# ConvFFN of a hybrid decoder layer: a small product that nothing reads, of eleven kinds in turns, behind every tenth group of projection matmuls

## The chip, the cores and the metric

The kernel runs on one core of one Trainium2 chip. The metric is the device time of one execution in microseconds, as the median of several runs. A core has five engines that run side by side and meet through semaphores: TensorE (PE) multiplies matrices and writes to PSUM, VectorE (DVE) and ScalarE (ACT) compute element by element, GpSimd (POOL) does small copies and issues DMAs, SyncE (SP) issues DMAs. PEld is the part of TensorE that loads the stationary operand (the weights) of a product ahead of its turn.

## The reference

One inference step of one layer, for a prompt of 256 tokens and for 8 samples of 4 tokens; 256 + 32 = 288 token columns go through the projections together. The layer has a Mamba-2 branch and a gated linear attention branch, a merge, cross-attention into 256 memory tokens, and a causal ConvFFN. The change touches the last part alone:

```python
up = _rmsnorm(h, p['norm_ffn']) @ p['w_up']                 # 2048 -> 2 * 5632
up, ffn_conv_new = _causal_dwconv(up, ffn_conv, p['ffn_conv_w'], p['ffn_conv_b'])
a, gt = jnp.split(up, 2, axis=-1)
h = h + (jax.nn.silu(gt) * a) @ p['w_down']                 # 5632 -> 2048
```

All weights and results are fp32. The outputs are y for both groups of tokens, the new convolution and recurrent states and the memory keys and values.

## The kernel before, in words

Every projection goes through `proj_w`. It takes a strip of 256 output channels (two groups of 128, `j`), walks over the inner dimension in tiles of 128 rows, and adds into two PSUM tiles `acc`, each 128 channels by 288 tokens. The weights come as 512 KB loads (`raw`, three buffers, issued by SP). `wsplit` turns each pair of tiles into two fp32r parts: `hi` by a cast on ScalarE (L102, tile whi) and `lo`, the rest, by a subtraction on VectorE (L104, tile wlo), with five buffers each. The activations are split in the same way (hf for the up-projection, pr for the down-projection).

One step of the generator is one pair of inner tiles. For each of the two groups `j` it makes six products of 128 weight columns by 288 token columns: hi by high part (L134) and hi by low part (L135) for both inner tiles, then lo by high part (L138) for both. So a step is 12 products, in the order 134 135 134 135 138 138, twice. At the end of a step the generator yields.

The ConvFFN is a loop over six blocks of channels. `ffn_up` runs the strips of w_up of a block (inner dimension 2048, 8 steps each), and as each strip ends `ffn_conv` does the convolution on VectorE, ScalarE and GpSimd; `ffn_down` runs the 8 strips of w_down for the block before (4 steps each, 2 for the first and smaller block). `flush` puts work that was set aside, such as the transposes of the convolution caches (L1540), into a strip's second half; in the last block `tail_rows` (L1619) transposes finished rows for the output. PSUM has eight banks: four for acc, three for `mm`, one for `la`, which cross-attention used last.

The kernel asks for a schedule that is made with a simulated timeline; `tc.keep_in_program_order` ties an instruction to its place among its engine's instructions.

Of the kernel before, what the change touches and what calls it, by code (L numbers as in the profile page):

```python
# [16 lines left out]
P = 128  # L17
# [24 lines left out]
def hybrid_step(ctx: ExitStack, tc: tile.TileContext, I: dict, O: list):  # L42
# [4 lines left out]
    MM, TR = nc.tensor.matmul, nc.tensor.transpose  # L47
# [12 lines left out]
    def acc_tiles(n):  # L60

        turn[0] += 1
        return [ps.tile([P, 512], F32, tag=f"acc{turn[0] % 2}", bufs=2, name="acc") for _ in range(n)]
# [4 lines left out]
    def la_tile():  # L68
        return ps.tile([P, 512], F32, tag="la", bufs=1, name="la")


    ident = const.tile([P, P], F32, name="ident")
    make_identity(nc, ident)
    ones = const.tile([P, P], F32, name="ones")
# [24 lines left out]
    def wsplit(raw):  # L99

        hi = wp.tile(list(raw.shape), F32R, tag="whi", bufs=WB, name="whi")
        S.copy(hi, raw)  # L102
        lo = wp.tile(list(raw.shape), F32R, tag="wlo", bufs=WB, name="wlo")
        V.tensor_tensor(lo, raw, hi, ALU.subtract)  # L104
        return hi, lo
# [4 lines left out]
        return raw  # L110

    late = []

    def flush():

        while late:
            late.pop(0)()

    def proj_w(load, ncol, X, nk, cons, N=T):

        nt = (ncol + P - 1) // P
        accs = acc_tiles(nt)
        for k0 in range(0, nk, 4):
            kn = min(4, nk - k0)
            raw = load(k0, kn)
            for s0 in range(0, kn, 2):
                hi, lo = wsplit(raw[:, s0:s0 + 2, :])
                for j in range(nt):
                    m = min(P, ncol - j * P)
                    a = accs[j][0:m, 0:N]  # L130
                    cs = slice(j * P, j * P + m)
                    for k in range(2):
                        xh, xl = X(k0 + s0 + k)
                        MM(a, hi[:, k, cs], xh, start=(k0 + s0 + k == 0), stop=False)  # L134
                        MM(a, hi[:, k, cs], xl, start=False, stop=False)  # L135
                    for k in range(2):
                        xh, xl = X(k0 + s0 + k)
                        MM(a, lo[:, k, cs], xh, start=False, stop=(k0 + s0 + k == nk - 1))  # L138
                    if k0 + s0 + 2 == nk:
                        cons(j, a)  # L140
                if k0 + s0 == min(4, nk - 2):
                    flush()
                yield

    def proj(w, c0, ncol, X, nk, cons, row0=0):
        def load(k0, kn):
            return wload(w[row0 + k0 * P:row0 + (k0 + kn) * P, c0:c0 + ncol].rearrange("(k p) n -> p k n", p=P))
        return proj_w(load, ncol, X, nk, cons)
# [41 lines left out]
    def halves(alloc, name):  # L190

        ts = [alloc(f"{name}{i}") for i in range(2)]

        def at(k, n=None):
            t, o = ts[k // 8], k % 8
            if n is None:
                return t[:, o, :], t[:, 8 + o, :]
            return t[:, o:o + n, :], t[:, 8 + o:8 + o + n, :]
        return at
# [52 lines left out]
    X = halves(bigr, "xn")  # L252
    with pool("p0") as p0:
# [227 lines left out]
        def dt_cons(j, a):  # L481
# [4 lines left out]
            V.tensor_tensor(lr3[64:80, :], a[64:80], lr3[64:80, :], ALU.subtract)  # L486

        run(proj_w(dt_load, 112, X, KT, dt_cons))

        def dt_prep():  # L490
# [737 lines left out]
    for q in range(4):  # L1228
        m = pc.tile([P, 4, T], F32, tag="mar", bufs=2, name="mar")
# [36 lines left out]
    def rstd_of():  # L1266
        ssq = mm_tile()
        MM(ssq[:, 0:T], ones, rst.pop(), start=True, stop=True)
        return rstd_from(pb, ssq[:, 0:T], D)
# [4 lines left out]
    for j2 in range(KT // 2):  # L1274
        def cons(j, a, j2=j2):
            added(hx[j2][:, j, :], 2 * j2 + j, a, vec("norm_cross"), hn, acc)
# [236 lines left out]
    rf = []  # L1513
    store = []

    def ffn_conv(ct, a, out, st, cache):
        if not rf:
            rf.append(rstd_of())
        u = pf.tile([P, SEQ], F32, tag="fu", bufs=3, name="fu")
        sp = pf.tile([P, NB, 6], F32, tag="fsp", bufs=4, name="fsp")  # L1520
        G.tensor_copy(sp[:, :, 0:2], st.rearrange("p (b k) -> p b k", k=2))
        V.tensor_tensor(u, a[:, 0:SEQ], rf[0][:, 0:SEQ], ALU.mult)
        V.tensor_tensor(sp[:, :, 2:6], a[:, SEQ:T].rearrange("p (b l) -> p b l", l=NL),
                        rf[0][:, SEQ:T].rearrange("p (b l) -> p b l", l=NL), ALU.mult)
        w2, wb = fcol[:, 2, ct:ct + 1], fcol[:, 3, ct:ct + 1]
        S.activation(out[:, 0:SEQ], u, ACT.Identity, scale=w2, bias=wb)
        S.copy(cache[:, 0:2], u[:, SEQ - 2:SEQ])
        S.copy(cache[:, 2:18].rearrange("p (b k) -> p b k", k=2), sp[:, :, 4:6])
        outs = out[:, SEQ:T].rearrange("p (b l) -> p b l", l=NL)
        V.tensor_scalar(outs, sp[:, :, 2:6], w2, wb, ALU.mult, ALU.add)  # L1530
        for k in range(2):
            s = 2 - k
            V.scalar_tensor_tensor(outs, sp[:, :, k:k + 4], fcol[:, k, ct:ct + 1], outs, ALU.mult, ALU.add)
            V.scalar_tensor_tensor(out[:, s:SEQ], u[:, 0:SEQ - s], fcol[:, k, ct:ct + 1], out[:, s:SEQ], ALU.mult, ALU.add)
# [16 lines left out]
    def ffn_up(b0, n):  # L1551
        pr = bigr2("pr")
        todo = []
        for q0 in range(b0, b0 + n, 4):
            st = fst[:, q0 // 4]
            ca = pf.tile([P, 18, 4], F32, tag="fca", bufs=3, name="fca")
            cg = pf.tile([P, 18, 4], F32, tag="fcg", bufs=3, name="fcg")
            for j2 in range(2):
                av = [pf.tile([P, T], F32, tag="av", bufs=4, name="av") for _ in range(2)]

                def consa(j, a, j2=j2, av=av, st=st):
                    t = 2 * j2 + j
                    ffn_conv(q0 + t, a, av[j], st[:, t, :], ca[:, :, t])

                def consg(j, a, j2=j2, av=av, st=st):
                    t = 2 * j2 + j
                    gv = pf.tile([P, T], F32, tag="gv", bufs=3, name="gv")
                    ffn_conv(FT + q0 + t, a, gv, st[:, 4 + t, :], cg[:, :, t])
                    S.activation(gv, gv, ACT.Silu)
                    V.tensor_tensor(gv, gv, av[j], ALU.mult)  # L1570
                    kk = q0 - b0 + t
                    split(pr[:, kk, :], pr[:, BLK + kk, :], gv)
                c0 = (q0 + 2 * j2) * P
                run(proj(I["w_up"], c0, 256, hf, KT, consa))
                run(proj(I["w_up"], FF + c0, 256, hf, KT, consg))
            todo += [(q0 * P, ca), (FF + q0 * P, cg)]
        store.append(todo)
        return pr
# [117 lines left out]
```

## Time and profile before

| what | value |
| --- | --- |
| median of 3 runs | 2575.54 us (2574.52 to 2577.21) |
| the profiled execution's own time | 2580.14 us |
| its span | 2578.4 us |
| mean granted TensorE clock | 0.998 |
| HBM read, written | 464.74 MB, 45.48 MB |

How to read the rows: a group of instructions begins with its line, engine and operation, then the tile it writes and those it reads, the array's rows and columns, the moving operand's shape and the count; behind the bar stand busy time in us, the mean length of one in ns, and the engine's idle time just before. A timeline row begins with its start and its length in us, counted from the span's start; rows of the same kind that follow each other are merged (x2). Lengths of products overlap, since the array is pipelined. A row of a table by stretches gives the stretch, its length, the busy time and count of each engine, the granted clock, the share of the DMA engines and GB/s. A row of the table of waits says which instruction waited for which, and total, times and longest in us.

### The profile page before, as it was taken

The page shows a single profiled execution, that of the slowest core. Times are in us where ns is not written, and L with a number is a line of the kernel's source. Part 1 is how long each engine was busy: PE and PEld are TensorE (multiplying, and loading weights), DVE is VectorE, ACT ScalarE, POOL GpSimd, SP SyncE. Part 2 cuts the span into 40 slices and gives each one's busy share as a digit, 9 for nine tenths or more (in the row PEclk, how much of TensorE's full clock was granted, in tenths as well). Part 3 has the DMA queues.
Part 4 walks back from the last instruction along what each step waited for, and adds up shares of the span by engine and source line. Part 5 has one row for each costly group of instructions (what it writes and reads, how often), then busy time and mean ns, then how long its engine had stood idle before and what let it go on. Part 6 is the DMA issues. An engine that isn't in the chain of part 4 may idle for free.

```text
span 2578.4 us, 50476 instructions
## 1 busy us (share of the span) xinstructions
PE 2560.9 (99%) x19119; PEld 2461.9 (95%) x19119; DVE 1712.0 (66%) x3623; ACT 1375.2 (53%) x2751; POOL 268.5 (10%) x519
## 2 busy tenths in 40 slices
PE   9999999999999999999999999999999999999998
PEld 7889999999999999999999989899999999999998
DVE  5656767687767666766666555567777676675765
ACT  6655647665464554544555444455545455454545
POOL 3002102120000000010000232200010001010000
PEclk9999999999999999999999999999999999999999
DMA  7766666666668585877666788755555555555553
GB/s 251 226 211 195 182 195 207 194 204 196 178 187 288 175 257 163 247 234 235 188 209 209 253 265 283 226 164 164 170 170 164 174 170 169 168 169 165 170 168 127
DMA packets 435203, 513.53 MB, mean 199 GB/s; under 512 B 23216, under 2 KB 385072, under 8 KB 434896
## 3 DMA queue, kind: packets, MB, share of 16 engines
q1 hardware_dynamic: 407568, 422.34, 53.1%
q0 software_dynamic: 27360, 87.96, 10.6%
q8 instruction: 150, 2.46, 0.4%
q14 instruction: 93, 0.76, 0.1%
q10 hardware_dynamic: 32, 0.01, 0.0%
HBM read 464.74 MB, written 45.48 MB: 198 GB/s over the span
## 4 chain that ended last, share of the span: by engine, by line
PE 97%; DMA 1%; ACT 0%; DVE 0%; issue 0%; SPq 0%; DVEq 0%; ACTq 0%
PE acc L135 27%; PE acc L134 27%; PE acc L138 27%; PE acc L316 2%; PE acc L317 2%; PE acc L320 2%; PE mm L1324 1%; PE la L1436 1%; PE la L1373 1%; PE la L1111 1%; PE mm L1120 1%; PE mm L851 1%; PE mm L1084 1%; DMA raw<-in_w_cv_dram 1%; DMA raw<-in_w_gla_out_dram 0%; DMA sin<-in_state_gla_dram 0%
## 5 line engine op out<-in xcount | busy, mean ns | idle before, releaser
L104 DVE TENSOR_TENSOR wlo<-raw,whi 128x512 fp32r<-128x512 f32 x1464 | 1001.6, 688 | 685.1 <-ACT whi L102 663.8
L102 ACT CAST whi<-raw 128x512 fp32r<-128x512 f32 x1464 | 900.0, 618 | 1023.1 <-PE acc L135 851.8
L134 PE MATMUL acc<-xn,whi 128*128 128x288 f32 (+1 forms) x1936 | 552.7, 301 | 0.0
L135 PE MATMUL acc<-xn,whi 128*128 128x288 f32 (+1 forms) x1936 | 540.7, 295 | 0.0
L138 PE MATMUL acc<-xn,wlo 128*128 128x288 f32 (+1 forms) x1936 | 414.7, 295 | 0.0
L135 PE MATMUL acc<-hf,whi 128*128 128x288 f32 x1408 | 391.9, 294 | 0.0
L134 PE MATMUL acc<-hf,whi 128*128 128x288 f32 x1408 | 390.0, 292 | 0.0
L134 PEld LDWEIGHTS acc<-xn,whi 128*128 128x128 f32 (+1 forms) x1936 | 363.7, 188 | 9.1 <-issue 7.7
L135 PEld LDWEIGHTS acc<-xn,whi 128*128 128x128 f32 (+1 forms) x1936 | 364.0, 188 | 5.7 <-issue 3.8
L138 PEld LDWEIGHTS acc<-xn,wlo 128*128 128x128 f32 (+1 forms) x1936 | 310.6, 188 | 0.3
L138 PE MATMUL acc<-hf,wlo 128*128 128x288 f32 x1408 | 298.8, 293 | 0.0
L135 PEld LDWEIGHTS acc<-hf,whi 128*128 128x128 f32 x1408 | 264.5, 188 | 0.1
L134 PEld LDWEIGHTS acc<-hf,whi 128*128 128x128 f32 x1408 | 264.2, 188 | 0.1
L138 PEld LDWEIGHTS acc<-hf,wlo 128*128 128x128 f32 x1408 | 225.4, 188 | 0.0
L135 PE MATMUL acc<-pr,whi 128*128 128x288 f32 x704 | 196.3, 295 | 0.0
L134 PE MATMUL acc<-pr,whi 128*128 128x288 f32 x704 | 195.9, 294 | 0.0
L138 PE MATMUL acc<-pr,wlo 128*128 128x288 f32 x704 | 149.1, 293 | 0.0
L134 PE MATMUL acc<-un,whi 128*128 128x288 f32 x512 | 145.8, 301 | 0.3 <-ACT whi L102 0.3
L135 PE MATMUL acc<-un,whi 128*128 128x288 f32 x512 | 143.1, 295 | 0.0
L135 PEld LDWEIGHTS acc<-pr,whi 128*128 128x128 f32 x704 | 132.3, 188 | 0.0
L134 PEld LDWEIGHTS acc<-pr,whi 128*128 128x128 f32 x704 | 132.1, 188 | 0.0
L138 PEld LDWEIGHTS acc<-pr,wlo 128*128 128x128 f32 x704 | 112.9, 188 | 0.0
(515 smaller groups left out, 4187.2 us busy)
## 6 DMA issues: line engine op xcount, KB each, us to landing
raw<-in_w_in_dram SPq DMA_DIRECT2D x240, 512.0 KB
raw<-in_w_up_dram SPq DMA_DIRECT2D x176, 512.0 KB
raw<-in_w_down_dram SPq DMA_DIRECT2D x88, 512.0 KB
raw<-in_w_ck_dram SPq DMA_DIRECT2D x32, 512.0 KB
raw<-in_w_cv_dram SPq DMA_DIRECT2D x32, 512.0 KB
raw<-in_w_ssd_out_dram SPq DMA_DIRECT2D x32, 512.0 KB
sin<-in_state_gla_dram POOLq DMA_DIRECT2D x32, 512.0 KB, 5.8
out_dram<-sin SPq DMA_DIRECT2D x32, 512.0 KB
```

What stands on the lines that cost most here:

```text
L102: S.copy(hi, raw)
L104: V.tensor_tensor(lo, raw, hi, ALU.subtract)
L134: MM(a, hi[:, k, cs], xh, start=(k0 + s0 + k == 0), stop=False)
L135: MM(a, hi[:, k, cs], xl, start=False, stop=False)
L138: MM(a, lo[:, k, cs], xh, start=False, stop=(k0 + s0 + k == nk - 1))
L316: MM(accs[m], mn_hi[:, kk, ms_], hi[:, 0, :], start=(kk == 0), stop=False)
L317: MM(accs[m], mn_lo[:, kk, ms_], hi[:, 0, :], start=False, stop=False)
L320: MM(accs[m], mn_hi[:, kk, ms_], lo[:, 0, :], start=False, stop=(kk == KT - 1))
L851: TR(a[:, t * P:(t + 1) * P], sin[:, e, t * P:(t + 1) * P], ident)
L1084: MM(a, kt[:, i, k * P:(k + 1) * P], vt[i], start=True, stop=True)
L1111: MM(osa[NS * j:NS * j + NS, :], qdm[:, k, b, :], sins[b][:, k, :], start=False, stop=(q == 1 and k == 0))
L1120: MM(a, kb[:, k * P:(k + 1) * P], vst, start=True, stop=True)
```

## The change

A list `nudge` is made beside `late`. At the end of each step, `proj_w` calls the function in it, if there is one, with the step's `hi` and the high part of the activations. The function `small` is put into the list ahead of the ConvFFN, so that projections ahead of it are not touched. It counts steps, and at every fifth (ten groups of six products) takes the next entry of a table of twelve, eleven of which differ. An entry names a kind, a width and a number of repeats. Kind 0 transposes `ident` (fp32; 72 or 128 columns, once or twice). Kind 1 multiplies `ones` with `ident` as weights in plain fp32 (8, 16 or 32 columns). Kind 2 multiplies a part of the activations with the step's `hi` as weights in fp32r (16, 40, 64 or 100 columns). All write into `junk`, a tile in the bank of `la`, which nothing reads.

```diff
@@ -110,6 +110,7 @@
     late = []
+    nudge = []
 
     def flush():
 
@@ -140,6 +141,8 @@
                 if k0 + s0 == min(4, nk - 2):
                     flush()
+                if nudge:
+                    nudge[0](hi, X(k0 + s0)[0])
                 yield
 
@@ -1513,6 +1516,29 @@
     store = []
 
+    junk = la_tile()
+    count = [0, 0]
+    kinds = [(0, 72, 1), (2, 16, 1), (0, 72, 2), (1, 8, 1), (0, 128, 1), (2, 64, 1), (1, 16, 1), (0, 72, 2), (2, 40, 1),
+             (0, 128, 2), (1, 32, 1), (2, 100, 1)]
+
+    def small(hi, x):
+
+        count[0] += 1
+        if count[0] % 5:
+            return
+        k, n, m = kinds[count[1] % len(kinds)]
+        count[1] += 1
+        for _ in range(m):
+            if k == 0:
+                d = TR(junk[0:n, 0:P], ident[:, 0:n], ident)
+            elif k == 1:
+                d = MM(junk[:, 0:n], ident, ones[:, 0:n], start=True, stop=True)
+            else:
+                d = MM(junk[:, 0:n], hi[:, 0, 0:P], x[:, 0:n], start=True, stop=True)
+            tc.keep_in_program_order(d)
+
+    nudge.append(small)
+
     def ffn_conv(ct, a, out, st, cache):
```

In the changed kernel L134, L135 and L138 are L135, L136 and L139, and the small work stands at L1533 (transposes), L1535 (fp32) and L1537 (fp32r). On PE, at the end of the fifth step of the ConvFFN's first strip, stands in the kernel before:

```order
L134 MATMUL acc<-hf_20087,whi 128x288
L135 MATMUL acc<-hf_20087,whi 128x288
L138 MATMUL acc<-hf_20087,wlo 128x288 x2
L134 MATMUL acc<-hf_20087,whi 128x288
L135 MATMUL acc<-hf_20087,whi 128x288
```

and in the changed one:

```order
L135 MATMUL acc<-hf_20087,whi 128x288
L136 MATMUL acc<-hf_20087,whi 128x288
L139 MATMUL acc<-hf_20087,wlo 128x288 x2
L1533 MATMUL la<-ident 72x128
L135 MATMUL acc<-hf_20087,whi 128x288
L136 MATMUL acc<-hf_20087,whi 128x288
```

The transpose stands between the last product of one step and the first of the next; what is around it kept its order. Five steps later on PE, the first of the fp32r kind:

```order
L136 MATMUL acc<-hf_20086,whi 128x288
L139 MATMUL acc<-hf_20086,wlo 128x288 x2
L1537 MATMUL la<-hf_20086,whi 128x16
L135 MATMUL acc<-hf_20086,whi 128x288
```

It reads whi of the step that just ended, which before was last read by L135's products of that step. On POOL and SP no instruction moved; on VectorE some of the convolution's instructions and wlo's subtractions stand a few places earlier or later among each other.

## The prediction

> **What bounds the kernel now.** I read the page first: the span, the busy shares, the granted clock and the chain of waits.
>
> ```profile
> span 2578.4 us, 50476 instructions
> PE 2560.9 (99%) x19119; PEld 2461.9 (95%) x19119; DVE 1712.0 (66%) x3623; ACT 1375.2 (53%) x2751; POOL 268.5 (10%) x519
> PEclk9999999999999999999999999999999999999999
> PE 97%; DMA 1%; ACT 0%; DVE 0%; issue 0%; SPq 0%; DVEq 0%; ACTq 0%
> L135 PE MATMUL acc<-hf,whi 128*128 128x288 f32 x1408 | 391.9, 294 | 0.0
> ```
>
> TensorE is busy for 99% of the span, 97% of the chain is its own work, and the idle time ahead of the FFN's products (the last figure of the group) is 0.0. Whatever enters this stream lengthens it, unless it fits into a step that is paid already. A mean of 294 ns is no price: the products overlap. The price of one is the distance from start to start, so next I took the FFN in stretches and counted the products that write acc in each (the count stands behind PE's busy time).
>
> ```profile
> 1739.80:1882.70 142.90, 142.88 (x1084) 142.85 (x1085) 12.35 (x48) 0.00 (x0) 1.00 0.54 167
> 1884.40:2009.80 125.40, 125.40 (x966) 125.40 (x965) 15.04 (x47) 0.00 (x0) 1.00 0.55 170
> 2010.50:2160.10 149.60, 149.60 (x1151) 149.60 (x1152) 15.49 (x48) 0.00 (x0) 1.00 0.56 171
> 2160.80:2312.20 151.40, 151.40 (x1150) 151.40 (x1151) 15.53 (x48) 0.00 (x0) 1.00 0.55 169
> 2312.90:2464.30 151.40, 151.40 (x1150) 151.40 (x1151) 15.53 (x48) 0.00 (x0) 1.00 0.54 168
> 2464.90:2521.00 56.10, 56.05 (x431) 56.07 (x432) 8.16 (x18) 0.00 (x0) 1.00 0.54 172
> ```
>
> Each row is a stretch between two breaks of the stream by other PE work (the cache transposes of L1540, but for the ends). Divide length by count: 131.8, 129.8, 130.0, 131.7, 131.7 and 130.2 ns a product, at clock 1.00 in all six. So the same instructions run in two rhythms, about 130.0 and 131.7 ns, and each stretch keeps to one. Together 776.8 us for 5932 products, a mean of 131.0.
>
> **The change, part by part.** It takes nothing away. The FFN makes 44 strips of w_up with 8 steps and 8 strips of w_down with 22 steps in all: 528 steps of 12 products, 6336 products. Every fifth step adds small work, 105 times. The table of twelve entries runs through 8 times and then up to its ninth entry, which the order confirms: 45 transposes of 72 and 25 of 128 columns, 26 plain fp32 products (8, 16 or 32 columns), 35 fp32r products (16, 40, 64 or 100 columns), 131 in all. None waits for another engine's work of its own; each stands between two groups of projection products.
>
> *Transposes.* L1540 is the same instruction, 72 columns of weights and 128 moving, in the same stream:
>
> ```profile
> 2009.87 0.42 PE L138 MATMUL acc<-pr,wlo 128*128 128x288 f32 x2
> 2010.13 0.27 PE L1540 MATMUL mm<-ident,fca 128*72 128x128 f32 x1
> ...
> 2010.45 0.27 PE L1540 MATMUL mm<-ident,fcg 128*72 128x128 f32 x1
> 2010.48 0.38 PE L134 MATMUL acc<-pr,whi 128*128 128x288 f32 x1
> 2010.70 0.29 PE L135 MATMUL acc<-pr,whi 128*128 128x288 f32 x1
> ```
>
> From the start of the L138 pair to that of L135 are 0.83 us, of which three products take 0.39: four transposes cost 0.44, so 0.110 each. The start of L134 right behind (0.03 later) is early and its 0.38 long, so I measure to the product after it. A single one is no cheaper:
>
> ```profile
> 1884.12 0.42 PE L138 MATMUL acc<-pr,wlo 128*128 128x288 f32 x2
> 1884.37 0.27 PE L1540 MATMUL mm<-ident,fcg 128*72 128x128 f32 x1
> 1884.40 0.38 PE L134 MATMUL acc<-pr,whi 128*128 128x288 f32 x1
> 1884.61 0.30 PE L135 MATMUL acc<-pr,whi 128*128 128x288 f32 x1
> ```
>
> 0.49 less 0.39 is 0.10. For 128 columns the four transposes of L1324 stand between such rows too:
>
> ```profile
> 1504.76 0.43 PE L138 MATMUL acc<-hn,wlo 128*128 128x288 f32 x2
> 1505.03 0.60 PE L1324 MATMUL mm<-ident,kc 128*128 128x128 f32 x4
> 1505.38 0.38 PE L134 MATMUL acc<-hn,whi 128*128 128x288 f32 x1
> 1505.60 0.29 PE L135 MATMUL acc<-hn,whi 128*128 128x288 f32 x1
> ```
>
> (0.84 - 0.39) / 4 = 0.112. Seventy transposes at 0.11 are 7.7 us.
>
> *Plain fp32 products.* The nearest are L1453's, 32 columns against 128 columns of weights:
>
> ```profile
> L1453 PE MATMUL mm<-fold,os 128*128 128x32 f32 x32 | 3.9, 265 | 0.0
> 1500.10 0.97 PE L1453 MATMUL mm<-fold,os 128*128 128x32 f32 x8
> 1500.91 0.38 PE L134 MATMUL acc<-hn,whi 128*128 128x288 f32 x1
> 1501.13 0.29 PE L135 MATMUL acc<-hn,whi 128*128 128x288 f32 x1
> ```
>
> The program has 16 of these (four for each of four heads), the trace 32: two passes a product. From 1500.10 to 1501.13, less 0.13 for L134, are 0.90 us for 8 passes: 0.112 a pass. 26 products are 52 passes, 5.8 us.
>
> *Narrow fp32r products.* The trace has none. On the wide side stand one with 512 columns and one with 256:
>
> ```profile
> 784.01 0.40 PE L1120 MATMUL mm<-vst,kb 128*128 128x512 f32 x1
> 784.25 0.30 PE L134 MATMUL acc<-un,whi 128*128 128x288 f32 x1
> 1494.03 0.28 PE L1443 MATMUL mm<-pTh,vph 128*128 128x256 f32 x1
> 1494.14 0.30 PE L138 MATMUL acc<-hn,wlo 128*128 128x288 f32 x1
> ```
>
> 0.24 and 0.11 to the next start. On the narrow side L1453's pass: 0.112 with 32 columns. From 32 to 256 columns the price hardly moves, so what is common to them, 128 columns of weights, sets it. I take 0.115, 4.0 us for 35. The upper end is two passes as for plain fp32 (0.225, 7.9 us); the lower end is the 0.03 between two starts that the 1884.37 and 1884.40 rows show (1.1 us).
>
> Under "Back-to-back issue gap" the Trainium skill (TensorE: Matmul & The Clock Gate) gives start to start a floor of about 25 ns for up to 64 columns; under "LDWEIGHTS (loading the stationary operand)" it prices a weight load by columns over 1.2, 107 ns for 128. By the first alone the 52 passes and the 27 fp32r products of up to 64 columns would be about 2 us instead of 8.9, an estimate. L1453's 0.112 sides with the second; no row shows the floor in this stream.
>
> Sum of the added work: 7.7 + 5.8 + 4.0 = 17.5 us.
>
> *The rhythm.* Every small product is a break, and after a break the stream settles anew. There are now 105 stretches of 60 products. The nearest rows are the last block's, where L1619's six transposes break the stream after 48 products:
>
> ```profile
> 2521.26 0.82 PE L1619 MATMUL mm<-ident,h 128*128 128x128 f32 x6
> ...
> 2528.24 0.81 PE L1619 MATMUL mm<-ident,h 128*128 128x128 f32 x6
> ```
>
> 6.98 us less 6 x 0.11 over 48 is 131.7: the slow one. Of the five stretches that begin behind L1540, three were fast and two slow. I put the mean at 131.5, nearer the short stretches: (131.5 - 131.0) x 6336 = +3.2 us. The bounds are all fast, (130.0 - 131.0) x 6336 = -6.3, and all slow, +4.4.
>
> *What costs nothing.* The row of a whole stretch with all engines, and the longest wait of ScalarE from 1500 us on:
>
> ```profile
> 2030.00:2160.00 130.00, 130.00 (x1002) 130.00 (x1002) 91.60 (x217) 66.46 (x144) 6.66 (x16) 1.00 0.55 167
> ACT whi L102 <- PE acc L135: 433.3, 487, 2.9
> ```
>
> VectorE is busy 91.6 of 130 us, ScalarE 66.5, the DMA engines 55%. The cast that fills whi mostly stands waiting for PE to give a buffer back. The fp32r kind reads hi, so that buffer comes back two L138 products and one small product later: 2 x 0.13 + 0.11 = 0.37 us, 35 times. Queued behind that cast on ScalarE are the convolution's activations and casts, and VectorE's wlo waits for the cast. There are five buffers of some 1.57 us each (12 x 0.131), so the lead covers it; without it up to 35 x 0.37 = 13 us would be lost. VectorE's convolution and wlo instructions stand in a slightly other order, within that slack. Loads of weights gain time, since PE is what grows slower. The last la reader is long done when the junk tile takes that bank.
>
> Sum: 17.5 + 3.2 = 20.7 us. The profiled execution took 2580.14, so 2600.8 for its like; it lies 4.6 above the runs' median of 2575.54, to which I add the same: 2596.2.
>
> **The rivals.** *All fast.* Each kick leaves the stream at 130.0 ns. For it: three of the six long stretches; against it: L1619's. 17.5 - 6.3 = +11.2, 2586.7. Chance 0.18.
>
> *Two passes for narrow fp32r.* Each costs as a plain product: 35 x 0.11 = 3.9 more, 2600. For it: no narrow one is in the trace; against it: every fp32r group has one record a product. Chance 0.10.
>
> *Weight loads hidden.* The 79 narrow passes cost 0.03 each, as the rows at 1884.37 and 1884.40 seem to say: 7.7 + 79 x 0.03 + 8 x 0.115 = 11.0, with 3.2 for the rhythm +14.2, 2589.7. Against it: L1453's 0.112 a pass. Chance 0.05. (The floor that the Trainium skill states in TensorE: Matmul & The Clock Gate, under "Back-to-back issue gap", would have this effect.)
>
> *Faster.* The kick puts the stream into a rhythm not yet seen. In 2009.87 to 2010.13 two products take 0.26, or 130 each, so these rows show nothing quicker; it decides below 131.0 - 17.5/6.336 = 128.2 ns. At 127, (131.0 - 127) x 6336 = 25.3 saved less 17.5: 2567.7. For it: that there are two rhythms at all. Chance 0.03.
>
> *No effect.* The products that nothing reads are not executed: 2575.5. Against it: the order has all 131. With mixtures that end near there 0.04.
>
> **How the numbers follow.** The forecast keeps 0.60, from about 2592 (131.0, unchanged rhythm, is 2593.0) to 2599 (all slow at 131.7 with prices as taken is 2597.4). The range takes in all fast below and two passes with the slow rhythm above (17.5 + 3.9 + 4.4 = 25.8, 2601.3): 2587 to 2603. What is under 0.2% (5 us) cannot be told from nothing here. Faster 0.03; same 0.04; slower 0.93.
>
> **What would show it.** In the changed profile: TR's group (L1533) with 70 records, L1535 with 52, L1537 with 35, no idle time ahead of them or of the next product; 0.11 from neighbour to neighbour; acc products per stretch between 456 and 462 in 60 us once the small work's time is taken out; clock unchanged. I am wrong if the idle column of the FFN groups rises above 1 us, if L1537 costs twice L1533, or if the products between the kicks run outside 130.0 to 131.8.

## The result and the profile after

The changed kernel takes 2600.05 us (median of 4 runs, 2597.26 to 2601.77), the kernel before 2575.51 beside it: 24.5 us more, ratio 1.0085 with a 95% interval of 1.007 to 1.010. It is slower, as forecast (2596, range 2587 to 2603), by some 4 us more than the likeliest case.

The page of the changed kernel shows the same limit as before:

```profile
span 2600.0 us, 50783 instructions
PE 2583.9 (99%) x19276; PEld 2485.3 (96%) x19276; DVE 1713.7 (66%) x3623; ACT 1374.0 (53%) x2751; POOL 269.4 (10%) x519
PEclk9999999999999999999999999999999999999999
L135 PE MATMUL acc<-hf,whi 128*128 128x288 f32 x1408 | 399.3, 298 | 0.0
```

PE gained 157 records (19276 less 19119), the passes of the small work; the clock is the same and PE's products still wait for nothing (0.0 in the last row). The FFN's length can be read from the first start of its first group to the last start of the output's transposes. Before, then after (first and last start behind the three durations):

```profile
L134 PE MATMUL acc<-hf,whi x1408: 290/292/515, 1727.9 to 2459.3; 128*128 128x288 f32 x176
L1619 PE MATMUL mm<-ident,h x48: 270/272/329, 2521.3 to 2568.3; 128*128 128x128 f32 x48
```

```profile
L135 PE MATMUL acc<-hf,whi x1408: 290/293/509, 1724.0 to 2477.8; 128*128 128x288 f32 x176
L1645 PE MATMUL mm<-ident,h x48: 270/272/328, 2542.1 to 2589.9; 128*128 128x128 f32 x48
```

2568.3 - 1727.9 = 840.4 us before, 2589.9 - 1724.0 = 865.9 after: 25.5 us more. The spans differ by 21.6 only, because in this execution of the changed kernel the FFN began 3.9 us earlier; the part ahead of it varies like that between executions of one kernel too (1727.9 above and 1722.3 in the second profile of the kernel before).

The small work has the groups that the prediction named, and no idle time:

```profile
L1533 PE MATMUL la<-ident 128*72 128x128 f32 x45 | 9.3, 271 | 0.0
L1533 PE MATMUL la<-ident 128*128 128x128 f32 x25 | 5.5, 272 | 0.0
L1535 PE MATMUL la<-ones,ident 128*128 128x16 f32 x18 | 2.6, 221 | 0.0
L1537 PE MATMUL la<-hf,whi 128*128 128x64 f32 x7 | 1.4, 195 | 0.0
```

A narrow fp32r product, which had no row before, in the timeline:

```profile
1740.06 0.43 PE L139 MATMUL acc<-hf,wlo 128*128 128x288 f32 x2
1740.33 0.17 PE L1537 MATMUL la<-hf,whi 128*128 128x16 f32 x1
1740.36 0.38 PE L135 MATMUL acc<-hf,whi 128*128 128x288 f32 x1
1740.57 0.30 PE L136 MATMUL acc<-hf,whi 128*128 128x288 f32 x1
```

Read as before, 0.51 us less three products (0.395) is 0.115 for 16 columns. Over all 105 places the same reading gives, in the mean of each kind, 0.107 to 0.117 for one pass and 0.219 to 0.229 for two, 17.7 us in sum. So 25.5 - 17.7 = 7.8 us are left for the rhythm, 1.2 ns for each of 6336 products: their mean went from 131.0 to 132.2. This is how two of the stretches between kicks look (a kick is one entry of the table; from the start of one to that of the next):

```profile
1764.76 0.27 PE L1533 MATMUL la<-ident 128*128 128x128 f32 x1
...
1772.93 0.20 PE L1537 MATMUL la<-hf,whi 128*128 128x64 f32 x1
```

```profile
1845.86 0.38 PE L1533 MATMUL la<-ident 128*72 128x128 f32 x2
...
1853.89 0.28 PE L1535 MATMUL la<-ones,ident 128*128 128x8 f32 x2
```

8.17 us less 0.11 for the transpose are 134.3 ns for each of 60 products; 8.03 less 0.226 are 130.1. Of the 94 undivided stretches of 60 products, the second half of 19 ran at 130.0, of 45 at 131.7 and of 30 at 134.4. The last of these rhythms occurs in no long stretch of the FFN before.

### The profile page after: what moved, and what is told of

Same layout as the page of the kernel before. It is cut to its first block, busy times and chain, and to the rows that moved or that the text cites. A ratio compares the mean times of both kernels' runs of the same rounds, so it can differ in the third digit from the quotient of the medians.

```text
span 2600.0 us, 50783 instructions
## 1 busy us (share of the span) xinstructions
PE 2583.9 (99%) x19276; PEld 2485.3 (96%) x19276; DVE 1713.7 (66%) x3623; ACT 1374.0 (53%) x2751; POOL 269.4 (10%) x519
## 4 chain that ended last, share of the span: by engine, by line
PE 98%; DMA 1%; ACT 0%; DVE 0%; issue 0%; DVEq 0%; ACTq 0%
PE acc L135 27%; PE acc L136 27%; PE acc L139 27%; PE acc L319 2%; PE acc L320 2%; PE acc L323 2%; PE mm L1327 1%; PE la L1439 1%; PE la L1376 1%; PE mm L1123 1%; PE la L1114 1%; PE mm L854 1%; PE mm L1087 1%; DMA raw<-in_w_cv_dram 0%; DMA raw<-in_w_cq_dram 0%; PE la L1533 0%
## 5 line engine op out<-in xcount | busy, mean ns | idle before, releaser
L135 PE MATMUL acc<-xn,whi 128*128 128x288 f32 (+1 forms) x1936 | 552.8, 301 | 0.0
L136 PE MATMUL acc<-xn,whi 128*128 128x288 f32 (+1 forms) x1936 | 540.8, 295 | 0.0
L139 PE MATMUL acc<-xn,wlo 128*128 128x288 f32 (+1 forms) x1936 | 414.8, 295 | 0.0
L135 PE MATMUL acc<-hf,whi 128*128 128x288 f32 x1408 | 399.3, 298 | 0.0
L136 PE MATMUL acc<-hf,whi 128*128 128x288 f32 x1408 | 393.9, 295 | 0.0
L135 PEld LDWEIGHTS acc<-xn,whi 128*128 128x128 f32 (+1 forms) x1936 | 363.7, 188 | 9.0 <-issue 7.7
L136 PEld LDWEIGHTS acc<-xn,whi 128*128 128x128 f32 (+1 forms) x1936 | 364.0, 188 | 5.7 <-issue 3.8
L139 PEld LDWEIGHTS acc<-xn,wlo 128*128 128x128 f32 (+1 forms) x1936 | 310.7, 188 | 0.3
L139 PE MATMUL acc<-hf,wlo 128*128 128x288 f32 x1408 | 300.3, 295 | 0.0
L136 PEld LDWEIGHTS acc<-hf,whi 128*128 128x128 f32 x1408 | 265.2, 188 | 0.1
L135 PEld LDWEIGHTS acc<-hf,whi 128*128 128x128 f32 x1408 | 264.7, 188 | 0.2
L139 PEld LDWEIGHTS acc<-hf,wlo 128*128 128x128 f32 x1408 | 225.9, 188 | 0.0
L135 PE MATMUL acc<-pr,whi 128*128 128x288 f32 x704 | 200.5, 299 | 0.0
L136 PE MATMUL acc<-pr,whi 128*128 128x288 f32 x704 | 196.9, 295 | 0.0
L139 PE MATMUL acc<-pr,wlo 128*128 128x288 f32 x704 | 150.5, 295 | 0.0
L135 PE MATMUL acc<-un,whi 128*128 128x288 f32 x512 | 145.9, 301 | 0.0
L136 PE MATMUL acc<-un,whi 128*128 128x288 f32 x512 | 143.2, 295 | 0.0
L136 PEld LDWEIGHTS acc<-pr,whi 128*128 128x128 f32 x704 | 132.6, 188 | 0.0
L135 PEld LDWEIGHTS acc<-pr,whi 128*128 128x128 f32 x704 | 132.4, 188 | 0.0
L1547 POOL COPY fsp<-fst 128x16 f32<-128x16 f32 x88 | 37.6, 430 | 743.6 <-DVE av L1559 338.4
```

## The experiments

In each, the FFN's length is read from the same two groups, since in two executions of one kernel it repeated within 0.3 us where the whole time does not.

**The kernel before once more.**

> The kernel before, unchanged, with a second profile. If a stretch's rhythm follows from the program (what broke the stream, and the rhythm before it), the FFN's six long stretches come out as in the first profile: 131.7, 130.0, 130.0, 131.7, 131.7, 130.0 ns a product, and the time within 0.2% of 2575.5 us. If the rhythm is drawn by chance at each break, the six come out in another pattern and the FFN's length differs by some us.

Time 2575.77, ratio 0.9996 (0.9985 to 1.0006).

```profile
L134 PE MATMUL acc<-hf,whi x1408: 290/292/515, 1722.3 to 2453.8; 128*128 128x288 f32 x176
L1619 PE MATMUL mm<-ident,h x48: 270/272/454, 2515.7 to 2563.0; 128*128 128x128 f32 x48
```

The FFN took 2563.0 - 1722.3 = 840.7 us, and its six long stretches came at 131.7, 130.0, 130.0, 131.7, 131.7 and 130.0 again. In the FFN the rhythm is no draw: the same program gave the same sequence.

That holds where PE waits for nothing. Ahead of the FFN stands a stretch of 1862 products (from 1191.4 us on in the first trace), in which one L134 starts late, by nothing to 0.65 us from trace to trace; in the first trace it waits for the cast of whi. Here is the part behind that place, up to which PE's work is the same in all kernels of this document: the kernel before, then the runs e7_two_singles and f2_recipe below.

```profile
1219.10:1436.90 217.80, 217.80 (x1657) 217.80 (x1656) 8.90 (x20) 6.54 (x16) 1.00 0.67 205
1214.90:1437.40 222.50, 222.50 (x1657) 222.50 (x1656) 8.88 (x20) 6.54 (x16) 1.00 0.63 201
1214.70:1429.80 215.10, 215.10 (x1656) 215.10 (x1656) 8.89 (x20) 6.52 (x16) 1.00 0.65 208
```

That is 131.4, 134.3 and 129.9 ns: the same products in three rhythms, 7.4 us apart. Of the 13 traces eight have 131.7 there, three 134.4 and two 130.0, and where the rhythm changes it does so at this product. So a product that starts late seems to choose the rhythm as a kick does, and part of what varies ahead of the FFN would be this.

**One kind alone, 64 columns or 16.** The table is cut to one entry; between the two runs only the width differs:

```diff
-    kinds = [(0, 72, 1), (2, 16, 1), ...
+    kinds = [(2, 64, 1)]
```

```diff
-    kinds = [(0, 72, 1), (2, 16, 1), ...
+    kinds = [(2, 16, 1)]
```

> Every fifth step the same fp32r product of 64 columns, 105 in all. In the changed kernel the stretches behind this kind ran at 134.4 ns. Theory (the kind of kick sets the rhythm): 105 x 0.113 = 11.9 us for the products and (134.4 - 131.0) x 6336 = 21.5 us for the rhythm, so 2609 us, slower than the changed kernel though it has fewer products. Rival (any break redraws the rhythm with the mean of the changed kernel, 132.2): 11.9 + 7.6, 2595 us.

> The same with 16 columns instead of 64, nothing else differs from the run with 64. In the changed kernel the stretches behind this kind ran at 131.7 ns. Theory: 105 x 0.118 = 12.4 us and (131.7 - 131.0) x 6336 = 4.4 us, so 2592 us, some 17 us below the run with 64 columns. Rival: 12.4 + 7.6, 2595.5 us, and within 1 us of the run with 64.

64 columns: 2607.63 us, ratio 1.0116 (1.0096 to 1.0135). 16 columns: 2592.68, ratio 1.0057 (1.0042 to 1.0072). One stretch of 250 us of each with the count of all of PE's products, 64 columns first:

```profile
1900.00:2150.00 250.00, 250.00 (x1869) 249.98 (x1869) 169.56 (x398) 122.89 (x266) 18.50 (x36) 1.00 0.52 161
```

```profile
1900.00:2150.00 250.00, 250.00 (x1906) 249.98 (x1905) 172.32 (x405) 125.41 (x273) 20.75 (x36) 1.00 0.53 165
```

The rows show 37 products fewer in the same time at the same clock, though each kernel has the same number of instructions. The FFN took 871.4 and 856.4 us. With 64 columns 89 of 94 stretches settled at 134.4, with 16 columns 93 of 94 at 131.7. The rival, one mean for any break, is refuted: 15 us lie between the two. The kernel with 105 products of 64 columns is slower than the change with its 157 passes.

**Pairs of transposes.**

```diff
-    kinds = [(0, 72, 1), (2, 16, 1), ...
+    kinds = [(0, 128, 2)]
```

> Every fifth step a pair of transposes of 128 columns, 210 in all. In the changed kernel six of eight stretches behind such a pair settled at 130.0 ns, with some products at 130.8 in the mean until then. Theory: 210 x 0.113 = 23.8 us for the transposes, the rhythm at about 130.4, (130.4 - 131.0) x 6336 = -3.8 us, so 2595.5 us. Rival (any break redraws, 132.2): 23.8 + 7.6, 2607 us.

2599.26 us, ratio 1.0082 (1.0066 to 1.0098); the FFN took 864.3, which is 23.6 more than in the second profile of the kernel before. This missed both numbers: the stretches took turns, 47 at 130.0 and 47 at 131.7, so the mean stayed about 131.0 and only the 23.8 us of transposes were left. What a kick does depends on the rhythm that it meets, too.

**The change without the kinds behind which 134.4 stood.**

```diff
-    kinds = [(0, 72, 1), (2, 16, 1), (0, 72, 2), (1, 8, 1), (0, 128, 1), (2, 64, 1), (1, 16, 1), ...
+    kinds = [(2, 16, 1), (2, 16, 1), (0, 72, 2), (1, 8, 1), (0, 128, 1), (2, 16, 1), (2, 16, 1), ...
```

> The changed kernel with three entries of the table (one transpose of 72, fp32r of 64, fp32 of 16 columns), behind which its stretches ran at 134.4 ns, replaced by fp32r of 16 columns. Theory: the passes fall by 9 (1 us), the stretches at 134.4 go to 131.7 or below, some 36 x 60 x 2.7 ns = 5.8 us: 17 to 19 us above the kernel before, instead of 22 to 25. Rival (the added time is not from the rhythm behind these kinds): 1 us less than the changed kernel.

2595.73 us, ratio 1.0073 (1.0059 to 1.0087), 17.7 us above the kernel before by the medians (2578.07 beside it); the FFN took 860.6 us, 5.3 below the change where the passes account for 1. Of its stretches of 60, 6 instead of 30 ran at 134.4. So with most of the third rhythm went 4.3 of the 7.8 us that the change paid above the prices of its instructions; the rest is what 131.7 and the 6 stretches left at 134.4 cost above the old mean of 131.0.

**Twelve widths by turns with 16 columns.**

```diff
-    kinds = [(0, 72, 1), (2, 16, 1), ...
+    kinds = [(2, 16, 1), (2, 8, 1), (2, 16, 1), (2, 24, 1), ... (2, 16, 1), (2, 128, 1)]
```

> Every fifth step an fp32r product, by turns of 16 columns and of one of twelve widths (8, 24, 32, 40, 48, 56, 64, 80, 96, 100, 112, 128). Theory A (each kick acts by the time that it takes off the stream's phase, so the width decides, and 16 brings the stream back to 131.7): the stretch behind a width is the same each time it comes, 134.4 behind 64 and 131.7 behind 40 and 100. Theory B (what decides is the place in the strip): stretches behind one width differ from round to round. 12.2 us for the products; with a third or so of the widths at 134.4 about 2577 + 12.2 + 4.4 + 3 = 2597 us.

2598.53 us (two runs), the FFN 857.7. Behind 64 columns all four stretches ran at 134.4, behind 112 three of four; behind 8, 24, 32, 40, 48, 56, 80, 96, 100 and 128 none did (40 stretches), and behind 16 none of 45. That a third of the widths would end at 134.4 was too many: two of twelve do, and not by size, as 56 and 80 lie on both sides of 64. The one stretch behind 112 at 131.7 is also the only one of the four whose kick met another rhythm: cache transposes had come 36 products earlier, and ahead of the kick six products take 0.78 us, 130.0 each, where the other three kicks of 112 met 131.7.

```profile
2484.63 0.29 PE L135 MATMUL acc<-pr,whi 128*128 128x288 f32 x1
...
2485.41 0.29 PE L135 MATMUL acc<-pr,whi 128*128 128x288 f32 x1
...
2486.19 0.21 PE L1540 MATMUL la<-pr,whi 128*128 128x112 f32 x1
```

So the width and the rhythm that it meets go a long way. The starts in the traces also show that 131.7 comes in two forms. At 130.0 and at 134.4 the distances between starts repeat with each group of six products (780 and 807 ns a group); at 131.7 they repeat only with the step of twelve (1580 ns), and the shortest distance, 127 to 128 ns, lies either in the step's first group or in its second. In the traces of the changed kernel, of e1_only64, e5_widths and e7_two_singles, 64 columns led to 134.4 in all 108 stretches that met 130.0, 134.4 or the first form, and in none of the four that met the second (one of these was still settling).

**Two products in all.** This shows a rhythm kept without further kicks. The table gives the step of the ConvFFN behind which each stands; the function `kick` makes the product in a buffer of `mm`:

```diff
+    kicks = {104: (2, 16, 1), 184: (2, 64, 1)}
...
+                kick(hi, X(k0 + s0)[0])
                 yield
```

> The kernel before with two small products in all, each early in one of the FFN's stretches that ran at 130.0 ns: an fp32r product of 16 columns with some 74 steps of its stretch left, and one of 64 columns with some 90 steps left. Theory (the stretch keeps the rhythm that a kick gives): 131.7 behind the first, 74 x 12 x 1.7 ns = 1.5 us, 134.4 behind the second, 90 x 12 x 4.4 ns = 4.8 us, and 0.23 us for the products, so the FFN from its first product to the last transpose goes from 840.6 us (two profiles of the kernel before) to 847 us; a few us more or less if the breaks behind them come out another way. Rival (the stream falls back to its own rhythm): 840.8 us.

2581.11 us, ratio 1.0021 (1.0012 to 1.003): two small products that nothing reads can be measured. By stretches, with the products that write acc:

```profile
1885.00:1893.60 8.60, 8.60 (x67) 8.56 (x66) 2.51 (x6) 0.00 (x0) 1.00 0.63 203
1893.80:2012.10 118.30, 118.30 (x899) 118.30 (x900) 12.36 (x41) 0.00 (x0) 1.00 0.52 165
2012.80:2020.50 7.70, 7.70 (x60) 7.67 (x59) 1.15 (x3) 0.00 (x0) 1.00 0.69 224
2020.70:2167.40 146.70, 146.70 (x1092) 146.68 (x1092) 14.18 (x45) 0.00 (x0) 1.00 0.51 162
2168.00:2319.50 151.50, 151.50 (x1152) 151.50 (x1151) 15.52 (x48) 0.00 (x0) 1.00 0.53 168
2320.10:2469.70 149.60, 149.60 (x1152) 149.60 (x1151) 15.50 (x48) 0.00 (x0) 1.00 0.54 170
```

The 16 columns stand between the first two rows, the 64 columns between the third and the fourth. 118.3 / 899 is 131.6 and 146.7 / 1092 is 134.3 ns, where the kernel before had 129.8 and 130.0 in the same places. The FFN took 2573.2 - 1728.4 = 844.8 us, not 847, since the stretch in the last row came out at 129.9 where before it ran at 131.7: what later breaks lead to shifted too. Whether that comes from the rhythm that they met or from the `mm` buffer that each kick takes, so that later transposes write other buffers, was not separated.

**Kicks in the good direction.** Four kernels put a few kicks into the kernel before, to bring its slow stretches to 130.0. The first:

```diff
+    kicks = {("gate_b", 2), ("ffn", 10), ("ffn", 277), ("ffn", 373)}
...
+            tc.keep_in_program_order(TR(junk[:, 0:P], ident, ident))
```

> The kernel before with four kicks in all instead of 105: one pair of 128-column transposes of ident early in each of four long stretches that ran at 131.7 ns (the second gate's projection with w_mix_out behind it, some 1670 products, and three stretches of the FFN with 1086, 1152 and 1152). With pairs at every fifth step such a pair turned 131.7 into 130.0 and 130.0 into 131.7, 53 and 46 times. Theory: a stretch keeps the rhythm that the kick gives it, so 5060 x 1.7 ns = 8.6 us saved, less 4 x 0.23 for the pairs and some 0.2 to settle: 7.5 us below the kernel before, provided that the breaks after the kicks leave the rhythm as before; if they turn fast stretches slow, as little as 2 us. Rival (the rhythm falls back by itself, or depends on where in the strip it is): within 1 us of the kernel before or slower by the 0.9.

2578.15 us, ratio 0.9997 (0.9987 to 1.0006): a miss. The FFN took 842.1 us. Its three kicked stretches:

```profile
1740.40:1882.80 142.40, 142.26 (x1057) 142.00 (x1056) 11.93 (x47) 0.00 (x0) 1.00 0.53 163
2163.50:2311.00 147.50, 147.31 (x1131) 147.07 (x1131) 14.61 (x46) 0.00 (x0) 1.00 0.54 168
2313.90:2461.50 147.60, 147.60 (x1122) 147.51 (x1121) 14.64 (x46) 0.00 (x0) 1.00 0.54 168
```

PE's busy time by its count gives 134.6, 130.2 and 131.6 ns. The third is less odd than it looks. In the kernel before that stretch ran at 131.7, but behind the second kick its cache transposes led to 130.0, and this is what the third pair met, twelve products in 2313.09 - 2311.53 = 1.56 us:

```profile
2311.53 0.29 PE L144 MATMUL acc<-pr,whi 128*128 128x288 f32 x1
...
2313.09 0.29 PE L144 MATMUL acc<-pr,whi 128*128 128x288 f32 x1
```

From 130.0 a pair led to 131.7 in the run of pairs too. It was the same in the fourth place, ahead of the FFN: the stretch, the one with the late product, ran at 130.0 already when its kick came, and at 131.7 behind it. The first two pairs both met 131.7 and led to 134.4 and to 130.0, which stays unexplained. Ahead of the next kernels I therefore put a product of 40 columns, and the pair five steps behind it.

```diff
+    kicks = {10: (2, 40, 1), 15: (0, 128, 2), 277: (2, 40, 1), 282: (0, 128, 2), 373: (2, 40, 1), 378: (0, 128, 2)}
```

> The kernel before with nine small products in all: in each of the three FFN stretches that ran at 131.7 ns an fp32r product of 40 columns, and five steps later a pair of 128-column transposes. Behind this order of kicks 13 of 16 stretches ran at 130.0 ns in the changed kernel and in the run without the 134.4 kinds. Theory: some 3100 products 1.7 ns shorter, 5.3 us saved, less 1.0 us for the small products: an FFN of 836.4 us instead of 840.6, if the breaks leave the other stretches as they are. Rival (a kick's outcome depends on more than the kind and the two kicks before): one or more of the three stretches stays at 131.7 or goes to 134.4, 840 us or above.

2575.45 us, ratio 1.0005 (0.9995 to 1.0015). The FFN took 839.7 us: two of the three stretches went to 130.0, the last stayed at 131.7, and the stretch of 966 behind the first turned slow. The rival held in part. The next two kernels answer to what this one left:

```diff
+    kicks = {10: (2, 40, 1), 15: (0, 128, 2), 102: (2, 40, 1), 107: (0, 128, 2), 277: (2, 40, 1), 282: (0, 128, 2),
+             373: (2, 40, 1), 378: (0, 128, 2), 383: (0, 128, 2)}
```

```diff
+    kicks = {277: (2, 40, 1), 282: (0, 128, 2), 373: (2, 40, 1), 378: (0, 128, 2), 383: (0, 128, 2)}
```

> The run with nine small products, and five more where it left long stretches at 131.7 ns: the 40 columns and the pair in the stretch of 966, and a second pair, five steps behind the first, in the last stretch of 1152 (at every fifth step a pair turned 131.7 into 130.0 53 times of 55). If both go to 130.0: some 1850 products 1.7 ns shorter, 3.1 us saved, less 0.57 us for five passes, an FFN of 837.1 us instead of 839.7, and against the kernel before 3.5 us less. Rival (the outcome of a kick in a new place is not known ahead): between 838 and 844 us.

> The kernel before with kicks in the last two slow stretches of 1152 alone (40 columns, a pair, and in the last a second pair), the stretch of 1086 left at 131.7 and the one of 966 behind it at 130.0 as before. If both go to 130.0: some 2100 products 1.7 ns shorter, 3.6 us saved, less 0.9 us for eight passes, an FFN of 837.9 us instead of 840.6. Rival as above: 839 us or more.

With kicks in four stretches: 2572.59 us, ratio 0.9982 (0.9974 to 0.9991). With kicks in the last two alone: 2573.88, ratio 0.9988 (0.9979 to 0.9996). The FFN of the first:

```profile
L149 PE MATMUL acc<-hf,whi x1408: 290/292/515, 1722.8 to 2451.1; 128*128 128x288 f32 x176
L1635 PE MATMUL mm<-ident,h x48: 270/272/421, 2512.9 to 2560.0; 128*128 128x128 f32 x48
```

837.2 us, and 837.9 for the other, as expected to 0.1 us. Behind its kicks all long stretches of the FFN run at 130.0. So 14 passes that compute nothing make this kernel 0.18% faster than the one before, and faster than the changed one by 28.7 us in the FFN.

## Why the prediction was right, and where it was off

*What bounds the kernel* held: PE at 99%, no idle time ahead of the FFN's groups, the clock unchanged.

*The prices* held. Predicted 7.7 + 5.8 + 4.0 = 17.5 us, measured 17.7. The narrow fp32r product, for which I took 0.115 between 0.03 and 0.225, costs 0.107 to 0.117. The rival of hidden weight loads and the rival of two passes are both refuted by its row. That "128 columns of weights" set this price stays argued: a transpose with 72 columns of weights costs 0.114 as well, and no run varied the weights of the other kinds.

*What costs nothing* held: the small work's groups show no idle time, the products' groups still 0.0, and the longer hold on whi cost nothing that the profile shows.

*The rhythm* is the term that was mis-sized. That a kick settles the stream anew was right; the size was off: I wrote +3.2 us with all slow, +4.4, as the bound, and it measured 7.8. The step that failed is "each stretch keeps to one" of two rhythms, 130.0 and 131.7. There is a third at 134.4, which no long stretch of the FFN before showed and which 30 of 94 stretches took. A sign of it stood in the first trace, in a short stretch ahead of the FFN that I had not looked at:

```profile
276.40:286.00 9.60, 9.60 (x72) 9.60 (x72) 0.45 (x1) 0.43 (x1) 1.00 0.62 173
```

72 products in 9.60 us, of which about one lies over the ends: some 134 to 135 ns. Of the signs named for being wrong, one, products outside 130.0 to 131.8 between the kicks, came true; the range held by luck, because it had room for a price of narrow products that was not needed. That a short stretch would mostly be slow, argued from the last block, was right in direction but came from another kind of break: the runs show that the kind counts, together with the rhythm that it meets.

*The rival "all fast"* did not occur with this table, but the kernel with kicks in four stretches has all long stretches of the FFN at 130.0, with 14 passes. *The rival "faster"* did not occur: no rhythm below 130.0 was seen in any run.

What is settled: in the FFN, where PE waits for nothing, the rhythm follows from the program, it lasts until the next break, and kicks that nothing reads change it (two products alone, 16 against 64 columns alone). What stays open: what within TensorE makes the rhythms, why 64 and 112 columns mostly lead to the slowest, and why a pair that meets 131.7 led to 134.4 once, to 131.7 in the last of the three stretches, and else nearly always to 130.0. No rule was found that gives a kick's outcome ahead; those of the last two kernels were chosen from what the runs before had shown.

## What to carry to other kernels

Where one engine sets the end, price an added instruction by the distance between the starts of its neighbours, from a row of the same kind in the same stream; then ask what it does to the products behind it. Count products per stretch of time: a long stream of equal instructions can run in several steady rhythms, and what breaks the stream last chooses one. Do not take the slowest rhythm seen for the slowest there is, and compare a change of this size by the stage's length in the trace, since the start of the program varies by more: some 1650 products there alone differed by 7.4 us between executions.

## What the runs showed of the hardware that was not expected

A stream of products of 128 weight columns by 288 columns ran at 130.0, 131.7 or 134.4 ns from start to start, at a granted clock of 1.00 and without idle time, for up to 1152 products on end (134.4 for up to 1092 in the FFN). One fp32r product of 64 columns, priced at 0.11 us, changed 130.0 to 134.4 for the 1092 products behind it, some 4.7 us. One product that started up to 0.65 us late, ahead of the FFN, was followed by 130.0, 131.7 or 134.4 for some 1650 products, one rhythm in one execution and another in another, in kernels with the same PE work up to there. In the FFN the sequence of rhythms in two executions of one kernel was the same, and the FFN's length 840.4 and 840.7 us, while the whole time of that kernel's runs ranged from 2571.92 to 2579.99 us.
